# An RWKV block's decay made feature-major with a scan, the state products by two heads in turn, and modulation chunks beside the r, k, v products

## The chip, the cores and the metric

The kernel runs on one core of a Trainium2 chip. The metric is the device time of one execution in microseconds (us); for the kernel before it is given as the median of three runs. TensorE (PE) multiplies matrices, VectorE (DVE), ScalarE (ACT) and GpSimd (POOL) work elementwise, SyncE (SP) issues the DMA transfers. Each engine runs its instructions in the order of its own queue and waits for the others by semaphores.

## The reference

A model block for 512 positions of width 1024: a modulation vector from the condition, a norm, one wide projection, dilated attention and an RWKV-7 mixer side by side, gates, and a convolutional feed-forward; a second block with a mixture of experts follows. The change lies in the RWKV mixer with 16 heads of 64 features, of which this is the part that counts:

```python
z = z + (z_prev - z) * mu
r, k, v, w_low, a_low, g_low = jnp.split(z, [...], axis=-1)
w_log = -jax.nn.softplus(-(w0 + jnp.tanh(w_low) @ w2).astype(f32)) - 0.5
decay = jnp.exp(-jnp.exp(w_log))
a = jax.nn.sigmoid((a0 + a_low @ a2).astype(f32))
kk = heads(k * k_k)
kk = kk / jnp.maximum(jnp.sqrt(jnp.sum(kk * kk, axis=-1, keepdims=True)), 1e-12)

def step(state, inp):
    r_t, w_t, k_t, v_t, aa_t, bb_t = inp
    sa = jnp.einsum('bhvk,bhk->bhv', state, aa_t)
    state = state * w_t[:, :, None, :] + sa[..., None] * bb_t[:, :, None, :] + v_t[..., None] * k_t[:, :, None, :]
    return state, jnp.einsum('bhvk,bhk->bhv', state, r_t)
```

The logarithm of the decay is a constant times (1 + tanh(half of w0 + tanh(w_low) w2)), so inside a chunk of 64 positions the products of decays are exponentials of running sums.

## The kernel before

The sequence of 512 is cut into 8 chunks of 64 positions. `rwkv_quarter(q, fw)` runs four times, each for four heads, which are two halves (`i2`) of 128 features, two heads each. A quarter has four parts.

First its fronts, one for each half. `th` (L610 to L613) holds tanh of `tw` times `w2q` for 512 positions by 256 features, positions on partitions, for the whole quarter: four fp32 products with a row of ones for w0, two ACT tanh, one DVE add of 1. Four fp32 products of `th` with the triangle `tri` give the running sums `cum`, features on partitions, and ACT makes Dp and Dh (their exponentials, L627, L628). One product of `a2q` (rows 64 to 127) gives `ta`. Then come the dense products k, r, v in this order, each 24 fp32r products of 512 columns (a weight is split by `split` into `hi`, a cast on ACT, and `lo`, a subtraction on POOL or DVE in turn). Behind k stand the squares `ksq` and their sums (`a<-c,tmp`), then max, root and reciprocal `rn` (DVE L657, ACT L658, DVE L659), its broadcast (`a<-c,rn`), `kkn` (L673), `ta` (L674), and the tiles AR (L676, L677) and BKf (L675). Sixteen fp32 products of BKf with AR follow, one for each chunk and head, each on 64 rows (`par` 0 or 1), and DVE multiplies them with masks into SA and SB (L691, L692).

Second the chain: the 32x32 blocks go to DRAM and back (`Ad`, `At`), DVE inverts them in 31 steps of two operations, and the inverse goes through DRAM again (`Td`, `TTh`, `Tq`); PE waits for it at `b<-inv`. Third the scan over the 8 chunks, a serial loop in which each chunk has three small groups on PE: `b<-X,SA`, `b<-Ps,TT`, `b<-X,SB`. Fourth the group norm of Y (tile `Ti`, L798 to L806), its transposes (`b<-c,Ti`) and the store.

Other work fills PE: `fw` is a chain of generators, `f_qk`, `f_v` (24 products of 256 columns for each piece, copied out as `stv`) and `f_gate`, that do the dense products of attention and gates; `pull(fw, n)` takes n pieces of it between the scan's steps. `fa` makes the modulation (`ada_group`): a chunk loads 1 MB of raw weight (`raw`, two buffers, shared with the other raw weights) and has eight fp32 products with 32 columns of output and 256 of input (`mm<-raw,c`), plus a DVE add into `rows`. Before, `run_fill` behind each quarter takes the rest of that quarter's `fw` in turn with five pieces of `fa`, for the quarters 1 and 2.

The program order is a list of priorities: a scheduler puts the instructions of each engine in order from it, with its own estimates of when operands are there. So code written behind the quarter stands in the engines' queues beside the chain and the scan of the same quarter, and fronts of the next quarter stand inside the scan. PSUM tiles: tag `a` and `b` three banks each, `mm` two.

Of the kernel before, what the change touches and what calls it, by code (L numbers as in the profile page):

```python
# [20 lines left out]
PVN = [('n1', 8), ('bada', 48), ('bgate', 16), ('mu', 24), ('mul0', 1), ('mul1', 1), ('mul2', 1), ('a0', 8),  # L21
# [28 lines left out]
def constants():  # L50
# [4 lines left out]
    tri = np.where(blk & (p[:, None] <= p[None]), -0.5 * EM5, 0.0)  # L55
# [5 lines left out]
    c1 = np.concatenate([tri, mA, blk, hs2], 1)  # L61
# [29 lines left out]
def layout(inp):  # L91
# [6 lines left out]
           'mul1': mu[3200:3280], 'mul2': mu[3280:3360], 'a0': g['a0'], 'kk': g['k_k'], 'ka': g['k_a'],  # L98
# [26 lines left out]
    A['w2a'] = np.ascontiguousarray(np.concatenate([g['w2'][0], g['w0']], 0))  # L125
# [36 lines left out]
def body(tc, I, O):  # L162
# [4 lines left out]
    with es:  # L167
# [8 lines left out]
        def G(tag="a"):  # L176
            return pp.tile([128, 512], F32, tag=tag, bufs=3, name=tag)
# [4 lines left out]
        def mm(out, l, r, start=True, stop=True):  # L182
            return nc.tensor.matmul(out, l, r, start=start, stop=stop, skip_group_check=True)  # L183

# [313 lines left out]
        c1 = rp.tile([128, 386], F32, name="c1")  # L498
        nc.sync.dma_start(c1, I['c1'])
        tri, mA, blk1, hs2 = c1[:, 0:128], c1[:, 128:256], c1[:, 256:384], c1[:, 384:386]  # L500
        dv = rp.tile([128, 52], F32, name="dv")
        omu, ka2, a0h, rkh, omul = dv[:, 0:24], dv[:, 24:32], dv[:, 32:40], dv[:, 40:48], dv[:, 48:51]
# [3 lines left out]
        nc.vector.tensor_scalar(a0h, V('a0'), 0.5, None, op0=OP.mult)  # L506
        nc.vector.tensor_scalar(rkh, V('rk'), 0.5, None, op0=OP.mult)
# [6 lines left out]
        tw = rp.tile([65, 512], F32, name="tw")  # L514
# [3 lines left out]
        nc.scalar.activation(tw[0:64], wl[0:64], AF.Tanh)  # L518
        nc.gpsimd.memset(tw[64:65], 1.0)
# [79 lines left out]
        def rwkv_quarter(q, fw):  # L599
            T = lambda shape, tag, bufs=1, dt=F32: (rpa if tag in EARLY else rp).tile(list(shape), dt, tag=tag, bufs=bufs, name=tag)  # L600
            w2q = T([65, 256], "w2q")
            nc.sync.dma_start(w2q, I['w2a'][:, 256 * q:256 * q + 256])
# [4 lines left out]
            th = T([128, 4, 256], "th")  # L607
            for t2 in range(2):
                ps = G()
                for t in range(2):  # L610
                    mm(ps[:, 256 * t:256 * t + 256], tw[:, 128 * (2 * t2 + t):128 * (2 * t2 + t) + 128], w2q)
                nc.scalar.activation(th[:, 2 * t2:2 * t2 + 2], ps.rearrange("p (a b) -> p a b", a=2), AF.Tanh, scale=0.5)
            nc.vector.tensor_scalar(th, th, 1.0, None, op0=OP.add)  # L613
# [4 lines left out]
            for i2 in range(2):  # L618
                i = 2 * q + i2
                ii = slice(128 * i2, 128 * i2 + 128)  # L620
                cum = G()
                for t in range(4):
                    mm(cum[:, 128 * t:128 * t + 128], th[:, t, ii], tri)
# [1218 lines left out]
```

## Time and profile before

| | us |
|---|---|
| median of three runs | 2034.93 |
| lowest, highest | 2030.18, 2035.95 |
| the profiled execution | 2040.78 |
| its span, first to last instruction | 2039.0 |
| PE busy | 1932.9 |
| DVE busy | 1146.4 |
| ACT busy | 728.3 |

The mean granted TensorE clock was 0.966 of full speed. RWKV and the fillers run from about 60 to about 740 us; attention, the feed-forward and the second block follow. On the page, the span is cut in 40 slices of 51 us, and each digit is the busy share in tenths; the row PEclk is the clock that PE was granted, in tenths. Matmuls overlap in PE's pipeline, so what a group costs is read from the start of one to the start of the next, not from its duration. An fp32 product is two records. In the rows an idle time in square brackets is the wait of the engine just ahead, with what ended it.

### The profile page before, as it was taken

What the parts mean: (1) busy time and instruction counts of PE and PEld (TensorE: products, weight loads), DVE (VectorE), ACT (ScalarE), POOL (GpSimd) and SP (SyncE); (2) the same over time, 40 slices, a digit from 0 to 9 for tenths busy, and PEclk for the clock granted to TensorE, in tenths of its full rate; (3) what the DMA queues carried; (4) which work ended last, traced back from release to release, by engine and by line L of the source; (5) the groups of instructions that cost most, each with busy time, mean ns of one, the idle gap of its engine ahead of it and who ended that gap; (6) DMA issues with size and microseconds to landing.
All of it is one profiled execution on the core that took longest, in us unless ns stands there. A gap on an engine that the chain in (4) does not pass through costs nothing. (4 is left out here: it accounts for less than half of the span.)

```text
span 2039.0 us, 28480 instructions
## 1 busy us (share of the span) xinstructions
PE 1932.9 (95%) x11085; PEld 1442.3 (71%) x11085; DVE 1146.4 (56%) x2232; ACT 728.3 (36%) x1261; POOL 436.8 (21%) x273
## 2 busy tenths in 40 slices
PE   7999999999999899999999989999999999599997
PEld 4788787787888767777887767777779667444553
DVE  4573573463437354557898873174430562467776
ACT  3533423342343243324333332354332452322222
POOL 1421311220232111131322322221111131122221
PEclk9999999997999999999999999999999899799998
DMA  7233244324234254244655544222233341699994
GB/s 298 78 105 104 80 120 146 117 95 122 92 104 166 81 199 163 95 166 145 199 194 181 181 160 147 92 90 82 89 114 104 98 181 40 241 421 424 424 423 195
DMA packets 100048, 334.11 MB, mean 164 GB/s; under 512 B 30212, under 2 KB 35080, under 8 KB 76360
## 3 DMA queue, kind: packets, MB, share of 16 engines
q1 hardware_dynamic: 97608, 323.89, 44.7%
q0 software_dynamic: 2304, 8.39, 1.1%
q8 instruction: 88, 1.44, 0.3%
q14 instruction: 48, 0.39, 0.1%
HBM read 304.98 MB, written 27.26 MB: 163 GB/s over the span
## 5 line engine op out<-in xcount | busy, mean ns | idle before, releaser
L231 POOL TENSOR_TENSOR lo<-raw,hi 128x1024 fp32r<-128x1024 f32 (+1 forms) x108 | 261.1, 2417 | 904.9 <-ACT hi L228 803.3
L228 ACT CAST hi<-raw 128x1024 fp32r<-128x1024 f32 (+1 forms) x215 | 222.3, 1038 | 368.5 <-PE mm L183 303.0
L183 PE MATMUL mm<-hl,hi 128*128 128x512 f32 x1008 | 333.3, 405 | 0.3 <-ACT stv L584 0.3
L183 PE MATMUL mm<-h,hi 128*128 128x512 f32 x784 | 248.3, 396 | 8.1 <-DVE u L1054 6.0
L231 DVE TENSOR_TENSOR lo<-raw,hi 128x1024 fp32r<-128x1024 f32 (+1 forms) x107 | 140.5, 1313 | 197.9 <-ACT hi L228 196.6
L183 PEld LDWEIGHTS mm<-hl,hi 128*128 128x128 f32 x1008 | 189.6, 191 | 42.1 <-issue 6.3
L183 PE MATMUL mm<-hl,lo 128*128 128x512 f32 x504 | 202.1, 401 | 0.0
L183 PEld LDWEIGHTS mm<-h,hi 128*128 128x128 f32 x784 | 146.5, 189 | 45.4 <-issue 12.3
L356 DVE SCALAR_TENSOR_TENSOR asum<-araw,cv,asum 128x256 f32<-128x256 f32 x224 | 151.5, 680 | 25.7 <-DMA araw<-in_wada 20.7
L183 PE MATMUL mm<-h,lo 128*128 128x512 f32 x392 | 153.9, 393 | 0.0
L183 PE MATMUL mm<-fm,hi 128*128 128x512 f32 x352 | 111.4, 397 | 6.1 <-ACT fm L1058 6.1
L183 PE MATMUL b<-h,hi 128*128 128x512 f32 x368 | 115.8, 392 | 0.0
L183 PE MATMUL mm<-gu,XT 128*64 128x512 f32 x512 | 113.2, 595 | 0.0
L183 PEld LDWEIGHTS mm<-hl,lo 128*128 128x128 f32 x504 | 96.0, 190 | 20.3 <-issue 2.2
L183 PEld LDWEIGHTS mm<-gu,XT 128*64 128x64 f32 x512 | 36.8, 138 | 73.0 <-issue 63.5
L183 PEld LDWEIGHTS mm<-h,lo 128*128 128x128 f32 x392 | 74.2, 189 | 15.8 <-issue 0.2
L183 PEld LDWEIGHTS mm<-fm,hi 128*128 128x128 f32 x352 | 66.7, 191 | 22.1 <-ACT fm L1058 6.5
L183 PEld LDWEIGHTS b<-h,hi 128*128 128x128 f32 x368 | 69.7, 190 | 14.7 <-issue 0.2
L183 PE MATMUL b<-h,lo 128*128 128x512 f32 x184 | 72.2, 392 | 0.0
L183 PE MATMUL mm<-fm,lo 128*128 128x512 f32 x176 | 69.2, 393 | 0.0
L893 ACT ACTIVATE sc<-sc,st 128x512 f32<-128x512 f32 (+3 forms) x96 | 56.3, 588 | 26.6 <-DVE st L891 22.3
L183 PE MATMUL mm<-hi,hl 128*128 128x256 f32 x384 | 57.6, 296 | 2.8 <-ACT stv L584 2.8
(522 smaller groups left out, 3554.1 us busy)
## 6 DMA issues: line engine op xcount, KB each, us to landing
gu<-in_wgu SPq DMA_DIRECT2D x32, 2048.0 KB, 15.0
araw<-in_wada SPq DMA_DIRECT2D x128, 256.0 KB, 3.3
dn<-in_wde SPq DMA_DIRECT2D x32, 1024.0 KB, 14.8
raw<-in_wup SPq DMA_DIRECT2D x22, 1024.0 KB, 4.8
raw<-in_wada SPq DMA_DIRECT2D x16, 1024.0 KB, 5.9
raw<-in_wg SPq DMA_DIRECT2D x16, 1024.0 KB, 5.0
raw<-in_wrkv SPq DMA_DIRECT2D x12, 1024.0 KB, 5.1
raw<-in_wqk SPq DMA_DIRECT2D x12, 1024.0 KB, 4.9
```

The lines of the kernel that those rows point to most:

```text
L183: return nc.tensor.matmul(out, l, r, start=start, stop=stop, skip_group_check=True)
L228: nc.scalar.copy(hi[:, :n], src)
L231: eng.tensor_sub(lo[:, :n], src, hi[:, :n])
L356: nc.vector.scalar_tensor_tensor(a, raw[:, k], c, a, op0=OP.mult, op1=OP.add)
L893: nc.scalar.activation(sc[:, :W], sc[:, :W], AF.Exp, scale=-1.0, bias=st[:, 0:1], accum_out=st[:, 1:2])
```

## The change

Three things.

The decay. `th` for a quarter and the products with `tri` go. Each half has one product of w2q with `tw` (64 rows) into `wps`, features on partitions, put in turn with the product of `a2q` (`in_turn`: each is issued behind the one ahead of it). ACT makes tanh with w0 as its bias, DVE adds 1 over 128x512 and runs a multiply-and-add scan over it with the mask `keep`, which is 0 at each chunk's first position, so that the sum starts anew there (the trace would name it SCALAR_TENSOR_TENSOR `th<-keep,th`). Dp and Dh take the constant as the exponential's scale.

The sixteen products of BKf and AR go through `in_turn` with the two heads alternating throughout.

The modulation's pieces in the quarters 1 and 2 are pulled in the loop over k, r, v, behind k and v of the first half and k, r, v of the second, and no longer by `run_fill`.

```diff
+        def in_turn(calls):
+            i = None
+            for out, l, r, kw in calls:
+                with tc.issue_after(i.ins) if i is not None else nullcontext():
+                    i = mm(out, l, r, **kw)
+            return i
...
-        tw = rp.tile([65, 512], F32, name="tw")
+        tw = rp.tile([64, 512], F32, name="tw")
+
+        keep = rp.tile([128, 512], F32, name="keep")
+        nc.gpsimd.memset(keep, 1.0)
+        nc.gpsimd.memset(keep[:, 0:512:64], 0.0)
...
-        def rwkv_quarter(q, fw):
+        def rwkv_quarter(q, fw, na):
...
-            th = T([128, 4, 256], "th")
-            for t2 in range(2):
-                ps = G()
-                for t in range(2):
-                    mm(ps[:, 256 * t:256 * t + 256], tw[:, 128 * (2 * t2 + t):128 * (2 * t2 + t) + 128], w2q)
-                nc.scalar.activation(th[:, 2 * t2:2 * t2 + 2], ps.rearrange("p (a b) -> p a b", a=2), AF.Tanh, scale=0.5)
-            nc.vector.tensor_scalar(th, th, 1.0, None, op0=OP.add)
...
-                cum = G()
-                for t in range(4):
-                    mm(cum[:, 128 * t:128 * t + 128], th[:, t, ii], tri)
+                wps, aps = G(), G()
+                in_turn([(wps, w2q[:, ii], tw, {}), (aps, a2q[64:128, ii], wl[64:128], {})])
+                cum = T([128, 512], "th")
+                nc.scalar.activation(cum, wps, AF.Tanh, scale=0.5, bias=w0h[:, i:i + 1])
+                nc.vector.tensor_scalar(cum, cum, 1.0, None, op0=OP.add)
+                nc.vector.tensor_tensor_scan(cum, keep, cum, 0.0, OP.mult, OP.add)
...
-                nc.scalar.activation(Dp, c3, AF.Exp)
-                nc.scalar.activation(Dh, c3, AF.Exp, scale=-1.0, bias=eps[:, 1:2])
-                aps = G()
-                mm(aps, a2q[64:128, ii], wl[64:128])
+                nc.scalar.activation(Dp, c3, AF.Exp, scale=-0.5 * EM5)
+                nc.scalar.activation(Dh, c3, AF.Exp, scale=0.5 * EM5, bias=eps[:, 1:2])
...
                         acc = MM()
                         dense(acc, next(rkv_it), H)
+                    pull(fa, na and (1 if i2 or s != 1 else 0))
...
-                    for c in range(4):
-                        for par in range(2):
-                            mm(pA[par][:, 128 * c:128 * c + 128],
-                               BKf[64 * par:64 * par + 64, 4 * c4 + c].rearrange("p a b -> p (a b)"),
-                               AR[64 * par:64 * par + 64, 4 * c4 + c].rearrange("p a b -> p (a b)"))
+                    in_turn((pA[par][:, 128 * c:128 * c + 128],
+                             BKf[64 * par:64 * par + 64, 4 * c4 + c].rearrange("p a b -> p (a b)"),
+                             AR[64 * par:64 * par + 64, 4 * c4 + c].rearrange("p a b -> p (a b)"), {})
+                            for c in range(4) for par in range(2))
...
-            rwkv_quarter(q, fq)
-            run_fill(fq, islice(fa, na))
+            rwkv_quarter(q, fq, na)
+            run_fill(fq)
```

The loop visits s = 1 (k), 0 (r), 2 (v), so `s != 1` in the first half are r and v.

What this does to the engines' queues is seen at three places. The rows below are instructions in the order of one engine (line, operation, output and operands, shape, count of equal neighbours); lines of the changed kernel are up to six higher.

PE, q0, from the first half's AR products to the second half's first products, before; `mm<-hl` are dense products, `hl` the normed input:

```order
L183 MATMUL a<-AR,BKf 128x128 x16
L699 MATMUL a<-c_66,v 128x128 x4
L183 MATMUL mm<-hl,hi 128x512 x2
L183 MATMUL mm<-hl,lo 128x512
...
L712 MATMUL a<-c_66,BKf 128x128 x8
L183 MATMUL a<-c_433,th 128x128 x4
L183 MATMUL a<-wl,a2q 128x512
```

The same place in the changed kernel:

```order
L182 MATMUL a<-AR,BKf 128x128 x9
L182 MATMUL mm<-hl,hi 128x512 x2
L182 MATMUL mm<-hl,lo 128x512
L182 MATMUL a<-AR,BKf 128x128 x7
L704 MATMUL a<-c_66,v 128x128 x4
...
L717 MATMUL a<-c_66,BKf 128x128 x4
L182 MATMUL a<-tw,w2q 128x512
L182 MATMUL a<-wl,a2q 128x512
```

Three dense products now part the AR products, and the pair of w2 and a2 stands where the `th` products and a2 stood.

PE at the end of q0's scan, from the last state products to the transposes of Y (tile Ti), before (between the rows around the dots stand further dense products, 41 in all):

```order
L183 MATMUL b<-X,SB_459 128x64 x2
L183 MATMUL mm<-hl,lo 128x512
L183 MATMUL mm<-hl,hi 128x512 x2
...
L183 MATMUL mm<-hl,hi 128x512
L811 MATMUL b<-c_66,Ti 128x128 x4
L183 MATMUL b<-sg,g2q 128x512 x2
```

and in the changed kernel, complete:

```order
L182 MATMUL b<-X,SB_462 128x64 x2
L182 MATMUL mm<-raw,c_80 32x256 x8
L182 MATMUL mm<-hl,hi 128x512 x2
L182 MATMUL mm<-hl,lo 128x512
L182 MATMUL mm<-hl,hi 128x512 x2
L182 MATMUL mm<-hl,lo 128x512
L182 MATMUL mm<-hl,hi 128x512
L816 MATMUL b<-c_66,Ti 128x128 x4
L182 MATMUL b<-sg,g2q 128x512 x2
```

The dense products here are of v in q1's first half; on ACT the changed kernel has, at this place,

```order
L720 COPY SA_459<-AR 64x8x64 x2
L807 ACTIVATE inv<-Ti 128x1024
L235 CAST hi<-raw 128x1024
L809 ACT_TABLE_LOAD
```

with the square of the norm (`inv<-Ti`) ahead of the cast of v's weights (`hi<-raw`).

PE at the start of q1's second half, before:

```order
L712 MATMUL a<-c_66,BKf 128x128 x8
L183 MATMUL a<-c_433,th 128x128 x4
L183 MATMUL a<-wl,a2q 128x512
L183 MATMUL a<-c_433,tmp 128x2 x4
L183 MATMUL mm<-hl,hi 128x512
L183 MATMUL mm<-hl,lo 128x512
...
L183 MATMUL a<-c_66,rn 64x128 x8
```

and in the changed kernel:

```order
L717 MATMUL a<-c_66,BKf 128x128 x4
L182 MATMUL a<-tw,w2q 128x512
L182 MATMUL a<-wl,a2q 128x512
L182 MATMUL mm<-hl,hi 128x512 x2
L182 MATMUL mm<-hl,lo 128x512
...
L182 MATMUL mm<-raw,c_80 32x256 x8
L182 MATMUL a<-c_433,tmp 128x2 x4
L182 MATMUL a<-c_66,rn 64x128 x8
L182 MATMUL mm<-hl,hi 128x512 x2
```

The sums of squares (`a<-c_433,tmp`) and the broadcast of `rn`, parted by twenty dense products before, are now neighbours behind a chunk of the modulation. In q2's first half the order is the same, chunk, squares, `rn`, and AR follows with one product between.

## Rows read from the trace of the kernel before

**Rows 1.** The page: busy time of PE; PE busy and granted clock in slices

```profile
PE 1932.9 (95%) x11085; PEld 1442.3 (71%) x11085; DVE 1146.4 (56%) x2232; ACT 728.3 (36%) x1261; POOL 436.8 (21%) x273
...
PE   7999999999999899999999989999999999599997
...
PEclk9999999997999999999999999999999899799998
```

**Rows 2.** What PE waited for in 60 to 720 us: total, times, longest

```profile
PE b L183 <- DMA inv<-Td: 8.6, 4, 5.5
...
PE mm L183 <- ACT stv L584: 3.2, 3, 2.2
...
PE b L811 <- DVE Ti L806: 0.8, 1, 0.8
```

**Rows 3.** Timeline of PE, 87.5 to 91.5 us: start, duration, engine, line, operation, records

```profile
88.33 1.06 PE L183 MATMUL a<-c,th 128*128 128x128 f32 x8
89.32 1.12 PE L183 MATMUL a<-wl,a2q 64*128 64x512 f32 x2
90.37 0.50 PE L183 MATMUL mm<-hl,hi 128*128 128x512 f32 x1
90.71 0.39 PE L183 MATMUL mm<-hl,lo 128*128 128x512 f32 x1
90.94 0.63 PE L183 MATMUL mm<-hl,hi 128*128 128x512 f32 x2
```

**Rows 4.** Timeline of PE, 64 to 73 us

```profile
64.17 2.21 PE L183 MATMUL a<-w2q,tw 65*128 65x256 f32 x8 [3.38 <-issue]
65.82 1.41 PE L183 MATMUL mm<-hl,hi 128*128 128x512 f32 x2
```

**Rows 5.** Stretches, PE on tile BKf: window, its length, busy (records), clock, DMA

```profile
109.99:111.07 1.08, 1.08 (x17) 1.00 0.06 23
111.07:111.50 0.43, 0.43 (x7) 1.00 0.00 0
111.50:113.14 1.64, 1.59 (x13) 1.00 0.00 0
```

**Rows 6.** Stretches: length, busy of PE, PEld, DVE, ACT, POOL, then clock, DMA

```profile
308.10:311.50 3.40, 3.40 (x11) 2.53 (x9) 0.48 (x2) 0.00 (x0) 0.00 (x0) 0.50 0.58 229
...
482.20:489.00 6.80, 6.80 (x48) 6.56 (x45) 1.38 (x4) 2.19 (x3) 0.00 (x0) 0.50 0.44 152
492.40:516.30 23.90, 23.90 (x108) 17.38 (x105) 4.59 (x13) 5.61 (x12) 0.00 (x0) 0.50 0.38 134
```

**Rows 7.** Timeline of PE, 304 to 312 us

```profile
305.10 2.21 PE L183 MATMUL b<-inv,SA 32*32 32x32 f32 x64 [1.07 <-DMA inv<-Td]
```

**Rows 8.** Timeline of DVE, 213 to 224 us, q0's norm

```profile
214.25 0.43 DVE L792 TENSOR_TENSOR Ti<-b,Ps 64x256 f32<-64x256 f32 x1 [0.29 <-PE b L183]
...
222.24 1.23 DVE L806 TENSOR_TENSOR Ti<-Ti,mn 128x1024 f32<-128x1024 f32 x1
```

**Rows 9.** Timeline of ACT, 213 to 224 us

```profile
219.26 1.04 ACT L228 CAST hi<-raw 128x1024 fp32r<-128x1024 f32 x1
```

**Rows 10.** Timeline of ACT, 218 to 258 us, q1's second half

```profile
244.41 1.28 ACT L627 ACT_TABLE_LOAD   x1
245.70 0.60 ACT L627 ACTIVATE Dp<-a 128x512 f32<-128x512 f32 x1
...
247.48 1.28 ACT L658 ACT_TABLE_LOAD   x1
```

**Rows 11.** Timeline of DVE, 218 to 258 us, q1's two halves

```profile
233.76 0.75 DVE L673 SCALAR_TENSOR_TENSOR kkn<-k,pv,a 128x512 f32<-128x512 f32 x1 [0.58 <-PE a L183]
...
236.35 0.17 DVE L677 COPY AR<-kkn 128x8 f32<-128x8 f32 x1
...
240.68 1.28 DVE L706 TENSOR_TENSOR BKf<-BKf,Dp 128x512 f32<-128x512 f32 x2
...
251.08 1.87 DVE L663 SCALAR_TENSOR_TENSOR tmp<-r,dv,km 128x512 f32<-128x512 f32 x1 [1.87 <-POOL km L649]
```

More of the change, by code (lines that the diff above doesn't have):

```diff
@@ L19 @@
 MAGIC = 1.5 * 2.0 ** 23
-PVN = [('n1', 8), ('bada', 48), ('bgate', 16), ('mu', 24), ('mul0', 1), ('mul1', 1), ('mul2', 1), ('a0', 8),
+PVN = [('n1', 8), ('bada', 48), ('bgate', 16), ('mu', 24), ('mul0', 1), ('mul1', 1), ('mul2', 1), ('a0', 8), ('w0', 8),
        ('kk', 8), ('ka', 8), ('rk', 8), ('lw', 8), ('lb', 8), ('n2', 8), ('cw0', 44), ('cw1', 44), ('cw2', 44),
@@ L54, in constants @@
     blk = (p[:, None] // 64 == p[None] // 64)
-    tri = np.where(blk & (p[:, None] <= p[None]), -0.5 * EM5, 0.0)
     s = p % 64
@@ L60, in constants @@
     c0 = np.concatenate([ident, ones], 1)
-    c1 = np.concatenate([tri, mA, blk, hs2], 1)
+    c1 = np.concatenate([mA, blk, hs2], 1)
     r, i = p // 32, p % 32
@@ L97, in layout @@
     src = {'n1': g['norm1_w'], 'bada': g['b_ada'], 'bgate': g['b_gate'], 'mu': mu[:3072], 'mul0': mu[3072:3200],
-           'mul1': mu[3200:3280], 'mul2': mu[3280:3360], 'a0': g['a0'], 'kk': g['k_k'], 'ka': g['k_a'],
+           'mul1': mu[3200:3280], 'mul2': mu[3280:3360], 'a0': g['a0'], 'w0': g['w0'], 'kk': g['k_k'], 'ka': g['k_a'],
            'rk': g['r_k'], 'lw': g['lnx_w'], 'lb': g['lnx_b'], 'n2': g['norm2_w'], 'cw0': g['conv_w'][0, 0],
@@ L124, in layout @@
     A['wg'] = _chunks(np.stack([t[j] for j in range(8) for t in (ga, gb)]), 2)
-    A['w2a'] = np.ascontiguousarray(np.concatenate([g['w2'][0], g['w0']], 0))
+    A['w2'] = np.ascontiguousarray(g['w2'][0])
     A['a2'] = g['a2'][0]
@@ L497, in body @@
         rp = rw.enter_context(tc.tile_pool(name="rw", bufs=1))
-        c1 = rp.tile([128, 386], F32, name="c1")
+        c1 = rp.tile([128, 258], F32, name="c1")
         nc.sync.dma_start(c1, I['c1'])
-        tri, mA, blk1, hs2 = c1[:, 0:128], c1[:, 128:256], c1[:, 256:384], c1[:, 384:386]
-        dv = rp.tile([128, 52], F32, name="dv")
-        omu, ka2, a0h, rkh, omul = dv[:, 0:24], dv[:, 24:32], dv[:, 32:40], dv[:, 40:48], dv[:, 48:51]
+        mA, blk1, hs2 = c1[:, 0:128], c1[:, 128:256], c1[:, 256:258]
+        dv = rp.tile([128, 60], F32, name="dv")
+        omu, ka2, a0h, rkh, omul, w0h = dv[:, 0:24], dv[:, 24:32], dv[:, 32:40], dv[:, 40:48], dv[:, 48:51], dv[:, 52:60]
         nc.vector.tensor_scalar(omu, V('mu'), -1.0, 1.0, op0=OP.mult, op1=OP.add)
@@ L506, in body @@
         nc.vector.tensor_scalar(a0h, V('a0'), 0.5, None, op0=OP.mult)
+        nc.vector.tensor_scalar(w0h, V('w0'), 0.5, None, op0=OP.mult)
         nc.vector.tensor_scalar(rkh, V('rk'), 0.5, None, op0=OP.mult)
@@ L517, in body @@
         shift(accs[0], 128, V('mul0'), omul[:, 0:1], wl)
-        nc.scalar.activation(tw[0:64], wl[0:64], AF.Tanh)
-        nc.gpsimd.memset(tw[64:65], 1.0)
+        nc.scalar.activation(tw, wl[0:64], AF.Tanh)
         for s in range(2):
@@ L597, in f_gate @@
                     yield
-        def rwkv_quarter(q, fw):
+        def rwkv_quarter(q, fw, na):
             T = lambda shape, tag, bufs=1, dt=F32: (rpa if tag in EARLY else rp).tile(list(shape), dt, tag=tag, bufs=bufs, name=tag)
-            w2q = T([65, 256], "w2q")
-            nc.sync.dma_start(w2q, I['w2a'][:, 256 * q:256 * q + 256])
+            w2q = T([64, 256], "w2q")
+            nc.sync.dma_start(w2q, I['w2'][:, 256 * q:256 * q + 256])
             a2q = T([128, 256], "a2q")
```

## The prediction, made before the changed kernel ran

> **What bounds the kernel now.** I read the page's busy line and slices first: TensorE (PE) is busy for 95% of the span, and its tenths stand at 9 from the second slice to the last but one with three dips [rows 1]. The reader should then look at what PE waits for in 60 to 720 us, where the changed code runs: the longest entry is 8.6 us in four waits, for the inverse of the 32x32 blocks that comes back by DMA at the end of DVE's chain, and the next that the change touches is 3.2 us for `stv`, the copy behind a group of f_v [rows 2]. So in these 660 us PE's own work is the time, and a transfer or a faster DVE can give back some 15 us at most. Third, the granted clock: PE's two levels are 2.4 and 1.2 GHz, and three stretches show 0.50, one of them 23.9 us long with PE busy throughout [rows 6]. Work there costs double. The rest, 740 us onward, is the same program in both kernels; I take it as unchanged.
>
> **Decay: what goes and what comes.** Before, each quarter has four products of w2 (1.65 us from the first to the next group's start, [rows 4]), and each half a group of `th` products, 88.33 to 89.32 = 0.99 us, and one `a2` product, to 90.37 = 1.05 us [rows 3]. Per quarter 1.65 + 2 x 0.99 + 2 x 1.05 = 5.73, for four 22.9 us. After, each half has one w2 and one a2 product of 512 columns each, on rows 0 to 63 and 64 to 127. Whether they run together is the question. The nearest row is the product of AR and BKf: while the two heads alternate, 8 instructions of 128 columns take 1.08 us [rows 5], what 4 instructions of the same columns on all rows take in [rows 3]. The pair then costs 1.05, with a switch 1.1, and where the order splits it (once, in q0's scan, by state products) 2.1: 7 x 1.1 + 2.1 = 9.8. **Saving 13.1 us**; if they don't overlap it is 22.9 - 8 x 2.1 = 6.1, and 15 at best. On DVE the +1 over 128x1024 becomes two over 128x512, and two scans come. No row shows a scan: I bound it by an elementwise operation of 128x512 at 0.75 and by the slowest such at 1.87 [rows 11], and take 1.2, between the two. It lies beside PE's dense products wherever they stand between the pair and the first use of Dp, and in the open at the start of q1's and q2's second half, below.
>
> In the Trainium skill, "DVE: opcode table, instruction layouts, handler registers and perf-mode slots", paragraph Feedback, the scan runs at half throughput; doubling a plain operation's 0.75 would give an estimate of 1.5 and add 0.3 to each of those two places, 0.6 us to the sum. No run shows it yet.
>
> **AR by two heads in turn.** Before, the sixteen products come as 1.08 us alternating, then 0.43 and 1.64 for the other eight, four of one head and four of the other [rows 5]. After, nine come, some dense products, then seven: the ninth by itself about 0.2, the seven at the alternating rate 0.95. So 3.15 becomes 1.08 + 0.2 + 0.95 = 2.25 plus 0.2 for breaking in and out of the dense products: 0.6 to 0.7 saved, eight times, 4.8 us. But DVE now does the first BKf product (half of the 1.28 us of two, [rows 11]) ahead of the last four masks, so the blocks leave for DRAM some 0.6 us later, and that chain is the one that PE waits for at `b<-inv` [rows 2]: 4 x 0.6 = 2.4 given back. **Net -2.4 us** (-4.8 if the inverse has slack, 0 if none of the saving reaches its start).
>
> **The modulation's chunks leave the scans.** Their work on PE is the same wherever they stand, so moving them is worth only what it does to waits and clock. In q2's scan before, PE has those chunks, small state products and hardly any dense products from 492.4 to 516.3, all at 0.50 [rows 6]. After, dense products of f_v and f_gate stand in that place. At full clock those 23.9 us of work take half: **-12 us**, at least 0. The 482.2 to 489.0 stretch behind the inverse's wait stays. In q1's and q2's scans PE waited for `stv` [rows 2] where the chunks and f_v share the two mm banks; of 3.2 I take **-2 us**.
>
> **What their new place costs.** The dense products that fill the scans were taken from the joints between the quarters, and there PE now meets chains that were covered. Four places, by the order:
>
> (1) End of q0's scan. From the sum into Y at 214.25 to the last product of the norm at 222.24 + 1.23 = 223.47 is 9.2 us [rows 8], and before 41 dense products, 0.23 each [rows 3], lay in it; the wait there was 0.8 us [rows 2]. After, one chunk (1.0) and seven dense products (1.6) lie there, and these seven need a cast (1.04, before at 219.26, [rows 9]) that ACT now does behind the norm's square. 9.2 - 2.6 = 6.6 open, less what was open before and what the shorter DVE queue gives: **+5.5**.
>
> (2) Second half of q1. Between the decay pair and the squares' products stand six dense products and a chunk, 2.4 us with the pair's own 1.1 = 3.5. ACT needs in the same time a table load (1.28), the tanh, ta, k, km2, Dp, Dh and the square, at some 0.6 each [rows 10]: 5.5 to 6. Open: 2.3. The next products, `rn`, follow without any dense product in between, and behind the square ACT loads the sqrt table again, 1.28 [rows 10], of which the squares' products cover 0.9: with max, root and reciprocal 1.0 open. Then r's lo part stands on DVE behind kkn (0.75, [rows 11]): 1.5. **+4.8** (2.7 if the table is there and the split is early, 5.5).
>
> (3) First half of q2: chunk, squares, `rn`, and straight to AR. The root's chain is open as in (2), with a DVE product of up to 1.87 [rows 11] ahead of the reciprocal: 2.4. Then kkn to the copy of AR, 233.76 to 236.35 + 0.17 = 2.8 [rows 11], has only one product of 1.1 in front of AR (before, eight dense products with it): 2.4 with the hops. **+4.9** (2.5 to 6).
>
> (4) Second half of q2, like (2): **+4.6** (2.7 to 5.5).
>
> Sum 19.8, from 13.4 to 22.5. **The clock behind these waits.** A wait of 1.07 us for the inverse [rows 7] was followed by 3.4 us at 0.50 from 308.1 on, and the inverse's wait in q2 by 6.8 us from 482.2 on [rows 6]. I take 3.4 us for each of the four places, at half speed a loss of 1.7: **+6.8** (0 to 13.6).
>
> **Sum.** -13.1 - 2.4 - 12 - 2 + 19.8 + 6.8 = -2.9 us. The profiled run took 2040.78 us, its span 2039.0, and stands 5.9 above the median of the three runs, 2034.93; a difference of -2.9 on either puts the median at 2032.
>
> **Rivals.**
> A, the joints cost less. If the clock stays at 1.0 behind the four waits (-6.8), and they take their lower bounds, 13.4 (-6.4), the sum is -16 and the time 2019. For it: a wait of 0.8 us before Ti [rows 2] had no slow slice behind it [rows 1]. Against: the order of ACT and DVE is fixed, so the waits at the joints are not a matter of luck.
>
> B, slower: the clock falls at the joints for longer. Chunk, squares and `rn` products of few columns now follow one another with waits between them, which is what the 23.9 us at 0.50 consisted of [rows 6]. If each joint brings 6.8 us at half clock (+6.8 over the forecast) and the 6 us or so of thin products at the two starts of second halves run at half clock as well (+6), the sum is -2.9 + 12.8 = +10, 2045. It decides from the point where the half-clock time gained at the joints passes the 24 us saved in q2's scan.
> The Trainium skill, "TensorE: Matmul & The Clock Gate", section HAM oscillation, says that waits between groups of matmuls let the clock fall, so that each next group starts at the slow level. By that rule all four joints pay, and B's first half holds. The stretch from 308.1 [rows 6] agrees for a wait of 1.07 us [rows 7].
>
> C, the pair doesn't run together. The two products of a pair are 512 columns long and only two, where AR's alternated eight times; then 13.1 becomes 6.1 and the time is 2039. For it: the eight AR products that came as four and four took 1.64 us in their main part, so two in a row of one head did not overlap with the other's [rows 5].
>
> D, the change does not lift the clock in q2's scan: state products of 64 columns stay and dense ones of 256 columns come between. Then 12 are missing: 2044. Against: q0's scan, with dense products between the same state products, keeps the clock at 9 tenths or more in its slices [rows 1].
>
> **How the numbers follow.** About 0.3%, 6.1 us, is what a measurement of this kernel tells from no change, so the bounds are 2028.8 and 2041.0. The forecast, 2032 with 2026 to 2038 by its single terms, has 0.44, of which 0.10 lies below 2028.8; A 0.24, B 0.16, C 0.08, D 0.08. Faster: 0.10 + 0.24 = 0.34. Same: 0.34 + 0.08 (C) = 0.42. Slower: 0.16 + 0.08 = 0.24. The range 2017 to 2045 leaves out about a third of A and half of B, and half of D's upper part.
>
> **What would show it.** In the profile after: the pair's two products starting within 0.1 us of each other and done in 1.1; AR in two runs, 1.1 and 0.95; q2's scan at a granted clock of 1.0; PE waits of 5 to 6 us at the end of q0's scan (before the transposes of Ti), and of 2 to 5 us ahead of `rn` and AR in q1's second half and both of q2's, each followed by 0.50 in the clock. The prediction is wrong if the joints show no waits, if the pair runs in 2.1, if half-clock time at the joints passes 20 us, or if the part from 740 us on differs by more than 3 us.

## The result and the profile after

The changed kernel is slower: median 2064.67 us of six runs (2057.4 to 2072.0) against 2034.3 of six runs of the kernel before, a ratio of 1.0133 with a 95% interval of 1.0093 to 1.0173. That is some 27 us by the ratio and 30 by the two medians. The forecast was 2032 with a range to 2045. The profiled execution took 2058.02 us, its span 2056.2. The first attention product (`po<-PT`), where the unchanged rest of the program begins, starts at 767.26 us, before at 743.93: 23.3 us later. The rest takes 1289.0 us after it, before 1295.0, with the same instructions: PE is at half clock, that is at a granted clock of 0.50, for 60.7 us of the rest, before for 82.1. The rest of the program isn't steady. It took 1295.3 us in a second trace of the changed kernel, and 1288.7 to 1302.1 over all traces of this document.

First the page of the changed kernel: PE is busy for 6.9 us less than in [rows 1] and a smaller share of a longer span; in the first half of the span the busy share falls in the fifth and the ninth slice, and the clock in the fifth, ninth, fourteenth and fifteenth.

```profile
PE 1926.0 (94%) x11005; PEld 1426.2 (69%) x11005; DVE 1169.6 (57%) x2245; ACT 729.5 (35%) x1261; POOL 436.6 (21%) x274
...
PE   7999799989999999999999989989999999699997
...
PEclk9999899989999889999999999999999999799999
```

What PE waited for in 60 to 760 us (total, times, longest), to be held against [rows 2]:

```profile
PE a L182 <- ACT tmp L652: 7.3, 3, 2.8
PE mm L182 <- ACT hi L235: 6.5, 2, 6.0
PE b L182 <- DMA inv<-Td: 6.1, 3, 4.4
PE a L182 <- DVE AR L683: 5.3, 4, 2.0
PE a L182 <- DVE bv L685: 5.3, 2, 2.7
PE mm L182 <- ACT stv L595: 5.0, 3, 3.3
PE a L182 <- DVE rn L665: 3.3, 4, 1.6
PE mm L182 <- DVE lo L238: 3.0, 2, 2.8
PE b L816 <- DVE Ti L811: 2.8, 3, 1.8
```

The wait for the inverse, the longest entry before, is now third. Above and around it stand waits inside the fronts: for the squares (`tmp` L652), a cast (`hi`), AR, `bv` (the bonus sums times v), `rn` and `lo`. Over the stretch from 60 us to the start of attention, before and then after (length, busy us of PE, PEld, DVE, ACT, POOL, then clock, DMA), PE is busy for the same time, and its idle time is 47.8 us instead of 24.1:

```profile
60.00:743.90 683.90, 659.78 (x4257) 537.95 (x4256) 358.19 (x710) 258.26 (x411) 144.87 (x84) 0.96 0.34 109
60.00:767.30 707.30, 659.50 (x4180) 528.16 (x4179) 377.62 (x710) 256.05 (x404) 144.44 (x84) 0.93 0.33 105
```

Then the stages of the changed kernel in the same columns, without those that the text doesn't read. The boundaries of all are the first w2 product of q1 (180.70), q1's AR products (235.01, 269.41), its inverse (324.28), its transposes of Y (385.07), the same for q2 (414.01, 461.11, 514.91, 573.55), q3's inverse (685.70) and attention.

```profile
180.70:235.01 54.31, 46.38 (x261) 32.77 (x260) 24.27 (x47) 18.59 (x31) 10.36 (x9) 0.91 0.21 75
235.01:269.41 34.40, 29.70 (x172) 21.24 (x172) 20.48 (x30) 17.43 (x24) 8.87 (x5) 0.85 0.39 131
269.41:324.28 54.87, 48.91 (x365) 45.50 (x364) 38.89 (x83) 14.29 (x24) 9.86 (x4) 0.96 0.45 132
...
414.01:461.11 47.10, 40.24 (x220) 28.45 (x221) 21.75 (x33) 18.72 (x26) 11.43 (x6) 0.86 0.41 140
461.11:514.91 53.80, 48.57 (x287) 41.80 (x286) 40.53 (x83) 13.89 (x21) 9.85 (x4) 0.97 0.43 131
514.91:573.55 58.64, 56.80 (x494) 51.65 (x495) 26.17 (x45) 22.24 (x43) 5.08 (x3) 0.97 0.19 61
...
685.70:767.26 81.56, 79.55 (x582) 60.70 (x582) 32.30 (x74) 26.82 (x53) 7.26 (x4) 0.82 0.27 91
```

and of the kernel before the two stages between the AR products, q2's scan and the last stage:

```profile
236.75:257.63 20.88, 19.68 (x124) 15.12 (x123) 14.50 (x25) 11.86 (x17) 6.27 (x4) 1.00 0.20 60
...
405.01:430.37 25.36, 24.71 (x146) 19.50 (x146) 13.41 (x25) 14.21 (x20) 8.63 (x5) 1.00 0.17 51
...
480.73:553.30 72.57, 70.51 (x523) 60.74 (x524) 27.66 (x49) 23.32 (x43) 7.45 (x4) 0.79 0.32 105
...
670.55:743.93 73.38, 70.69 (x589) 55.13 (x589) 32.82 (x80) 27.80 (x57) 7.45 (x4) 0.96 0.32 107
```

| stage | before, us (clock) | after, us (clock) |
|---|---|---|
| to q1's first w2 product | 124.54 (0.96) | 120.70 (0.96) |
| to q1's first AR | 52.21 (1.00) | 54.31 (0.91) |
| q1's first to second AR | 20.88 (1.00) | 34.40 (0.85) |
| to q1's inverse | 47.47 (1.00) | 54.87 (0.96) |
| q1's scan | 62.04 (0.97) | 60.79 (0.93) |
| to q2's first AR | 37.87 (1.00) | 28.94 (1.00) |
| q2's first to second AR | 25.36 (1.00) | 47.10 (0.86) |
| to q2's inverse | 50.36 (1.00) | 53.80 (0.97) |
| q2's scan | 72.57 (0.79) | 58.64 (0.97) |
| to q3's inverse | 117.25 (1.00) | 112.15 (1.00) |
| to attention | 73.38 (0.96) | 81.56 (0.82) |

q2's scan gave what was forecast, 13.9 us, with its clock back from 0.79 to 0.97. (What stands in a stage differs between the kernels: two chunks left this one and 18 dense products came in.) The stages from the first to the second AR of q1 and of q2 lost 13.5 and 21.7 us, of which the moved chunks and dense products are about half by their counts (two chunks of 1.07 us and 21 dense products of 0.23 more in q1, three and 31 in q2). Waits and a clock of 0.85 and 0.86 are the other half. The way from q1's second AR to its inverse lost 7.4, and the last stage 8.2.

The second front of q1, timeline of PE in the changed kernel, shows how one joint looks:

```profile
241.15 0.69 PE L182 MATMUL a<-tw,w2q 64*128 64x512 f32 x1
241.15 0.69 PE L182 MATMUL a<-wl,a2q 64*128 64x512 f32 x1
241.68 0.59 PE L182 MATMUL a<-tw,w2q 64*128 64x512 f32 x1
241.69 0.59 PE L182 MATMUL a<-wl,a2q 64*128 64x512 f32 x1
242.20 0.73 PE L182 MATMUL mm<-hl,hi 128*128 128x512 f32 x2
...
243.79 1.07 PE L182 MATMUL mm<-raw,c 128*32 128x256 f32 x16
247.50 1.64 PE L182 MATMUL a<-c,tmp 128*128 128x2 f32 x8 [2.64 <-ACT tmp L652]
249.87 1.97 PE L182 MATMUL a<-c,rn 128*64 128x128 f32 x16 [0.73 <-DVE rn L665]
252.41 1.22 PE L182 MATMUL mm<-hl,hi 128*128 128x512 f32 x2 [0.57 <-ACT hi L235]
...
270.50 0.50 PE L182 MATMUL mm<-hl,hi 128*128 128x512 f32 x1
273.65 0.48 PE L182 MATMUL a<-AR,BKf 64*128 64x128 f32 x2 [2.64 <-DVE bv L685]
```

The pair of w2 and a2 starts together and is done in 1.05 us, as forecast. Then come a chunk, a wait for ACT, the squares, a wait for the root, `rn`, a wait for a cast; and at the ninth AR product one of 2.64 us for `bv`, which no step of the prediction had. On DVE the modulation's own last operation (`ada`, L310, 2.10 us from 270.04) stands ahead of v and `bv` there, and in q2's second half likewise (2.10 us from 461.74).

### The profile page after: what moved, and what is told of

It reads as the page before. It is cut to its first block, busy times and chain, and to the rows that moved or that the text cites. A ratio compares the mean times of both kernels' runs of the same rounds, so it can differ in the third digit from the quotient of the medians.

```text
span 2056.2 us, 28313 instructions
## 1 busy us (share of the span) xinstructions
PE 1926.0 (94%) x11005; PEld 1426.2 (69%) x11005; DVE 1169.6 (57%) x2245; ACT 729.5 (35%) x1261; POOL 436.6 (21%) x274
## 5 line engine op out<-in xcount | busy, mean ns | idle before, releaser
L182 PE MATMUL mm<-hl,hi 128*128 128x512 f32 x1008 | 347.1, 418 | 11.0 <-ACT hi L235 6.5
L363 DVE SCALAR_TENSOR_TENSOR asum<-araw,cv,asum 128x256 f32<-128x256 f32 x224 | 154.2, 691 | 23.4 <-DMA araw<-in_wada 18.8
L734 DVE TENSOR_TENSOR Ti<-Ti,Ps 64x31 f32<-64x31 f32 (+15 forms) x124 | 58.4, 471 | 4.2
```

What stands on the lines that cost most here:

```text
L363: nc.vector.scalar_tensor_tensor(a, raw[:, k], c, a, op0=OP.mult, op1=OP.add)
L734: nc.vector.tensor_sub(Ti[:, 0:s + 1, s + 1:32], Ti[:, 0:s + 1, s + 1:32], m)
```

## The experiments

Ratios are to the kernel before on the same chip, with 95% intervals; 1% is 20 us. The median of the kernel before lay between 2034.3 and 2042.2 us on these chips, so kernels are compared by their ratios rather than by their times. In this section the chain is the inverse's, as in the part on the kernel before.

| kernel | ratio | interval |
|---|---|---|
| all three parts (the change) | 1.0133 | 1.0093 to 1.0173 |
| the change again | 1.0136 | 1.0081 to 1.0192 |
| decay and AR, chunks as before | 0.9970 | 0.9938 to 1.0001 |
| chunks moved, nothing else | 1.0241 | 1.0188 to 1.0295 |
| decay alone | 0.9997 | 0.9966 to 1.0028 |
| AR in turn alone | 1.0104 | 1.0047 to 1.0160 |
| the change with spare products | 1.0144 | 1.0093 to 1.0194 |
| chunks in the chain, nothing else | 0.9938 | 0.9908 to 0.9968 |
| the same with AR | 0.9969 | 0.9943 to 0.9995 |
| the same with decay | 0.9897; 0.9920 | 0.9868 to 0.9926; 0.9892 to 0.9947 |
| the same with decay and AR | 0.9956; 0.9956 | 0.9937 to 0.9976; 0.9928 to 0.9985 |
| the same with decay ahead and AR | 0.9922 | 0.9890 to 0.9954 |
| the same with decay ahead | 0.9911 | 0.9879 to 0.9943 |
| chunks at q1's joints, q2's in the chain | 1.0035 | 1.0002 to 1.0068 |
| chunks at q2's joints, q1's in the chain | 1.0041 | 1.0011 to 1.0071 |

**The parts apart.** Theory 1: the chunks' new place makes the loss. Theory 2: the decay's longer way through ACT and DVE does.

Chunks put back:

```diff
-                    pull(fa, na and (1 if i2 or s != 1 else 0))
-            run_fill(fq)
+            run_fill(fq, islice(fa, na))
```

> The changed kernel with the modulation's chunks put back behind the quarters (the decay by scan and the AR products in turn stay). Theory 1, the moved chunks make the loss (they take the dense products out of the joints, PE waits there and its clock falls): this kernel is free of it and keeps the saving of the decay products, 13 us less about 4 us for the squares of q1's second half, which now stand right behind the w2 and a2 pair: 2020 to 2026. Half-clock time between 60 and 740 us 45 to 60 us as before, PE waits 20 to 26 us in all. Theory 2, the decay's longer chain through ACT and DVE (tanh, add, scan, exponentials) makes the waits wherever the chunks stand: 2045 to 2060, with waits on tmp of over 6 us and half-clock time over 70 us.

Measured 2034.65, ratio 0.997: 33 us (1.6%) better than the change, so theory 2 is out as the main cause. But it was expected at 2020 to 2026; decay and AR brought 0.3%, not 0.6. PE's idle time was 25.5 us, as expected, but the half-clock time 73 us instead of 45 to 60, with 27 us of it in q2's scan.

The kernel before with the reverse of this edit, that is the chunks' move alone:

> The kernel before with only the modulation's chunks moved beside r, k, v. Theory 1 (the chunks make the loss): 2055 to 2075, that is what the change lost plus what decay and AR give, with PE waits in 60 to 760 us of 40 us or more and half-clock time of 75 us or more. Theory 2 (the decay's chain makes the waits): 2025 to 2040, since here the decay is ready a quarter ahead; half-clock time falls to some 30 us because q2's scan keeps its clock.

2090.72, ratio 1.0241, beyond what theory 1 expected. PE's idle time in the RWKV part is 48.1 us, as in the change, and about 117 us of that part go at half clock; among the waits stand 8.3 us for `stv` and 7.8 for Ti. Here the decay is ready ahead, and the loss is larger. One part of the expectation failed: q2's scan, with no chunk in it, ran at half clock from 519.9 us on for 27.3 us, from within a wait of 4.07 us for `stv`. So moving the chunks out of a scan doesn't by itself keep its clock.

Decay alone (the `tri` and `th` lines of the diff, chunks and AR as before), then AR in turn alone:

> The kernel before with only the decay by scan. By the prediction's term 13 us are saved on PE, of which 4 go to a wait ahead of the squares in q1's second half: 2022 to 2027 by theory 1. By theory 2: 2045 or more. Beside the run with decay and AR it shows what AR in turn is worth: if more than 2 us, AR's saving reaches the end; if nothing or less, it is given back through the masks and the inverse's chain.

2037.05, ratio 0.9997: neither theory's number. Its profile has two stretches of 27 and 20 us at half clock in the scans of q1 and q2, where the chunks still stand (stage, PE busy, then clock at the end):

```profile
308.20:335.60 27.40, 26.89 (x162) 18.63 (x159) 6.79 (x17) 7.73 (x14) 2.35 (x1) 0.50 0.43 159
496.00:516.50 20.50, 19.34 (x90) 13.91 (x90) 4.25 (x11) 3.27 (x8) 0.45 (x1) 0.50 0.42 147
```

> The kernel before with only the AR products in turn. By the prediction 2.4 us faster (4.8 saved on PE, 2.4 given back by the later masks): 2030 to 2034. If the broken rows of dense products or a wait for the third PSUM bank cost more than that: 2035 to 2040.

2058.05, ratio 1.0104, a miss: slower than either expectation. Its profile has two such stretches of 30.7 us:

```profile
315.30:346.00 30.70, 29.78 (x170) 21.41 (x168) 4.94 (x15) 7.64 (x14) 2.36 (x1) 0.50 0.27 102
496.20:526.90 30.70, 28.01 (x167) 20.43 (x166) 4.99 (x14) 6.37 (x15) 0.00 (x0) 0.50 0.32 109
```

Before, q1's scan lost it for 3.4 us only [rows 6]. With a small edit in the fronts, q1's scan with chunks in it fell to half clock as well. So the parts can't be priced with the chunks in the scans.

**Chunks in the chain.** To price them with the clock quieter, the chunks were placed among dense products while DVE inverts:

```diff
+            for j in range(na):
+                pull(fw, 12 if j == 0 else 4)
+                pull(fa, 1)
             At = T([64, 32, 32], "inv")
```

> The kernel before with only the chunks in the inverse's chain. Theory: the 24 us at half clock in q2's scan go, so 8 to 12 us faster than before, ratio 0.994 to 0.996; the distance to the kernel with decay and AR as well is what these two are worth once the clock holds, 10 to 16 us. Rival: same as before, 1.000, when the chunks among the chain's products bring waits of their own (raw weights by DMA, rows on DVE between the inverse's steps).

2025.0, ratio 0.9938: 0.6% from the chunks' place alone, a little more than was expected.

> Decay by scan and AR in turn, with the modulation's chunks pulled in the inverse's chain: behind the second half of q1 and q2 twelve pieces of f_qk, f_v, then one chunk, four pieces, one chunk and so on. Chunks then stand among dense products while DVE inverts, the joints have their dense products as before, and the scans of q1 and q2 hold dense products only. Theory (the clock in the scans and the waits at the joints decide, and the decay's 13 us are real): half-clock time in 60 to 760 us 25 to 40 us, PE waits 20 us, time 20 to 30 us below before, ratio 0.985 to 0.990. If the 13 us of the decay never reach the end: ratio 0.993 to 0.997, like the kernel with the chunks behind the quarters.

2025.85, ratio 0.9956: short of the 0.985 to 0.990, no better than the same without decay and AR. The clock wasn't as quiet as expected: 60 us at half clock instead of 25 to 40. Which of the two eats the gain was asked by leaving out one at a time: first the decay, then AR in turn.

> The kernel before with AR in turn and the chunks in the inverse's chain. AR in turn alone cost 1.0 per cent with the chunks behind the quarters, in a trace with 31 us at half clock in q1's scan and again in q2's. Theory: that was the clock in the scans, not AR; then this kernel is 0 to 4 us faster than the one with the chunks in the chain and the AR order of before, ratio 0.992 to 0.996. Rival: AR in turn costs by itself (broken dense groups, later masks): 10 us or more slower than that kernel, ratio 1.000 or more.

2028.7, ratio 0.9969: 0.3% slower than without AR in turn, between theory and rival, but the intervals overlap, so a cost isn't shown here.

> Decay by scan at each half's start, AR in the order of before, chunks in the inverse's chain. Theory: as the kernel with AR in turn, within 4 us, ratio 0.993 to 0.997; the distance to the kernel with the decay computed ahead is the price of the uncovered chain, 4 to 10 us. Rival: no distance, the waits at q1's second half are covered by time that would be lost at the inverse anyway.

2016.23, ratio 0.9897, the best of all. Against the kernel without the decay (0.9938, on another chip) it is worth 0.4%, 8 us of the 13.1, though the intervals overlap. Timed side by side in five rounds:

> Decay by scan, AR in turn, chunks in the chain, timed again beside the same with the AR order of before. If AR in turn costs: 6 to 12 us slower than that one (their separate medians were 2025.9 and 2016.2). If that distance was the chips' and the clock's chance: within 3 us of each other. By the prediction it would be 2.4 us faster.

> Decay by scan, the AR order of before, chunks in the chain: the best so far, ratio 0.9897. Expected again 0.988 to 0.993, 16 to 24 us below before.

2025.79 against 2019.14, ratios 0.9956 and 0.9920: with the decay by scan the kernel with AR in turn is some 7 us slower; the intervals overlap, the two separate comparisons agree in sign. But little of that lies where AR stands. In the two pairs of traces attention starts only 0.8 and 4.3 us later with AR in turn; the other 8.8 and 6.3 us fall in the unchanged rest, which has 90.5 and 83.3 us at half clock against 64.4 and 73.5. Whether the order of AR brings that isn't shown. What the traces do show is where the saving went. Timeline of PE in q1's second half, with AR in turn:

```profile
243.60 1.09 PE L182 MATMUL a<-c,rn 128*64 128x128 f32 x16
252.59 2.04 PE L182 MATMUL a<-tmp,c 128*128 128x512 f32 x2 [4.95 <-DVE tmp L668]
255.41 1.86 PE L182 MATMUL a<-AR,BKf 64*128 64x128 f32 x18
```

and with the AR order of before:

```profile
247.19 1.09 PE L182 MATMUL a<-c,rn 128*64 128x128 f32 x16
253.84 1.10 PE L182 MATMUL a<-tmp,c 128*128 128x512 f32 x2 [2.16 <-DVE tmp L668]
```

With AR in turn PE is 3.6 us ahead at `rn`, then waits 4.95 us instead of 2.16 for the bonus product that DVE and POOL make, and the clock falls (0.57 granted over 249 to 257 us), so that the products behind it take double. The saving on PE was real and was handed to a wait.

**The decay ahead.** That wait comes from the decay's way through ACT, so it was computed for both halves at the quarter's start (two buffers for `th` and `ta`):

```diff
+            for i2 in range(2):
+                wps, aps = G(), G()
+                in_turn([(wps, w2q[:, ii], tw, {}), (aps, a2q[64:128, ii], wl[64:128], {})])
...
+                cums.append(cum)
+                tas.append(ta)
```

> Decay by scan, AR in turn, chunks in the inverse's chain, and the w2 and a2 pairs, tanh, add and scan of both halves computed at the quarter's start instead of at each half's (two buffers for them; tanh of w_low is kept in place of w_low, the mask in bf16, to make room). Theory: in the kernel with the chunks in the chain what is left of the change's cost is the decay's chain through ACT and DVE, uncovered at q1's second half, where PE waited 4.9 us ahead of the bonus product. With it a quarter ahead, PE's waits fall by 4 to 6 us and the kernel is 4 to 10 us faster than that one: ratio to before 0.991 to 0.994, PE waits below 20 us, no wait over 2 us in q1's fronts. Rival: the decay's products are worth nothing at the end whatever covers them: 0.994 to 0.997.

> The same with the AR products in the order of before. The distance of the two is what AR in turn is worth with all else quiet. By the prediction 2.4 us (4.8 saved on PE, 2.4 given back by the later masks): this kernel 0 to 5 us slower than the one with AR in turn. Rival (AR in turn costs): this kernel 2 us or more faster.

2022.62 and 2023.15, ratios 0.9922 and 0.9911. With AR in turn the ratio is 0.3% lower than without the decay ahead, but the intervals overlap; the 4.9 us wait is gone, but one for AR of 3.7 us came, and PE's idle time is 22.4 us where less than 20 was expected. With the AR order of before it doesn't help: there the uncovered chain had no price, as the rival said. AR in turn is worth nothing here.

**The clock behind the waits.** The change with 68 dense products whose result nobody uses, put where PE waited:

```diff
+        def spare(n, i):
+            acc = G("b")
+            for j in range(n):
+                with tc.issue_after(i.ins):
+                    i = mm(acc, H[j % 8][0][:, 0:128], H[j % 8][0], start=(j == 0), stop=(j == n - 1))
+            return i
```

> The changed kernel with 68 spare dense products (their result is used by nobody) put where PE waited: 24 before the transposes of Y at the end of q0's scan, 10 behind the w2 and a2 pair of the second halves of q1 and q2, 6 between the squares and rn in all four fronts of these quarters. The order of all other instructions of PE stays. At full clock they are 68 x 0.23 = 15.4 us of work. Theory 1 (the granted clock that falls behind the waits costs about half of the loss): half-clock time between 60 and 760 us falls from 96 to 60 us or less, and the kernel, with more work, is 8 to 15 us faster than the changed one: 2050 to 2057 where before is 2034, a ratio to before of 1.008 to 1.012 or less. Rival (the waits alone are the loss, the clock follows chance): the same or up to 6 us slower than the changed kernel, ratio 1.013 to 1.017, since spare products that overrun a wait add time.

2067.39, ratio 1.0144: the rival's number. Half-clock time fell only to 75 us, not to 60, and the order didn't stay quite the same: at the end of q0's scan v's seven products now stand behind the transposes of Y. There the filling worked. The stretch 205 to 232 us, with the spare products and then in the change itself (the clock stands behind the five busy times):

```profile
205.00:232.00 27.00, 23.96 (x141) 16.59 (x140) 13.37 (x20) 9.83 (x14) 7.97 (x7) 1.00 0.34 111
```

```profile
205.00:232.00 27.00, 19.07 (x107) 11.91 (x106) 11.54 (x18) 9.72 (x13) 7.82 (x7) 0.81 0.30 105
```

The clock stays at 1.00 there instead of 0.81, and although PE has 30 products (6.8 us) more, q1's first AR comes 1.5 us sooner, counted from q1's first w2 product (52.86 against 54.31). So the waits there could be filled for nothing; whether the 1.5 us come from the clock or from the new order, this run can't tell. In q1's second half the clock fell all the same for 10 us, and with 16 spare products the way from the first to the second AR took 39.03 us instead of 34.40. Over the whole stretch attention starts at 767.67 us, in the change at 767.26: the spare work was paid for by 10.2 us less idle time and by 20 us less at half clock. My theory 1, that a quieter clock would make the kernel 8 to 15 us faster, isn't borne out. Waits and clock aren't two separate losses here: where PE runs faster it may wait longer for the same chain.

**Chance or order.** The changed kernel once more, without an edit.

> The changed kernel once more, on the chip of the others. Theory (the slow clock behind the joints belongs to the order, not to chance): half-clock time in 60 to 767 us again 85 to 105 us, with stretches of 3 us or more behind the same five joints (some 210, 248, 275, 439, 466 us), waits 45 to 50 us, ratio 1.010 to 1.016. Rival (chance): half-clock time below 70 us or at other places, ratio within 0.5 per cent of 1.

2059.58, ratio 1.0136, and 85 us at half clock, with stretches at 210, 245, 272, 320, 412, 436 and 463 us, all within 3.3 us of the first trace's; one of 3.4 us at 227 did not come again. So these belong to the order.

**One quarter at a time.** The pull at the joints for one quarter, in the chain for the other:

```diff
-                    pull(fa, na and (1 if i2 or s != 1 else 0))
+                    pull(fa, q == 1 and (1 if i2 or s != 1 else 0))
...
+            for j in range(0 if q == 1 else na):
+                pull(fw, 12 if j == 0 else 4)
+                pull(fa, 1)
```

> Decay by scan and AR in turn; q1's chunks beside its r, k, v products as in the change, q2's in the inverse's chain. With all chunks in the chain the ratio to before was 0.9956, with all at the joints 1.0133, 36 us apart. Theory (each joint is paid by itself: its waits and the slow clock behind them): about 60 per cent of that here, since q1 has the end of q0's scan besides its two fronts, 20 to 23 us, ratio 1.004 to 1.008. Rival (one place decides, say q2): within 8 us of one of the two ends.

> The mirror: q2's chunks at its joints, q1's in the chain. Theory: about 40 per cent of the 36 us, 13 to 17 us, ratio 1.001 to 1.005, and the excess of the two mixed kernels over the one with all chunks in the chain adds up to that of the changed kernel within 8 us. Rival: the two do not add up.

2043.61 and 2047.31, ratios 1.0035 and 1.0041. Over the kernel with all chunks in the chain (0.9956) that is 16 and 17 us, together 33; the change stands 36 over it. Each of the two has an uncertainty of some 7 us. Within it the quarters' losses add up; q1's share, expected at 20 to 23, is no larger than q2's. PE's idle time says the same: 35.0 and 35.4 us, between 23.4 with all chunks in the chain and 47.8 in the change.

## Why the prediction was wrong

PE's time from 60 us to attention can be split in three: its work as it would be at full clock, its idle time, and what the slow clock adds. The last is an estimate: half of PE's busy time in the half-clock stretches, which is 50.5 us of 51.1 before and 86.1 us of 95.2 after. It says what the slow clock took, and not what a steady clock would give back. The forecast's terms fall in the same three (of AR's -2.4, 4.8 are work saved and 2.4 a longer wait).

| | forecast, us | measured, us |
|---|---|---|
| work: decay, AR | -17.9 | -18.2 |
| PE's waits: joints, `stv`, inverse | +20.2 | +23.7 |
| slow clock | -5.2 | +17.9 |
| sum (rounded) | -2.9 | +23.3 |

So the work was right, the waits were nearly right in their sum, and the step that failed is the clock.

**The decay's products: right.** The pair takes 1.06 us at six of the seven places where it stands together and 1.13 at one, forecast 1.1, so rival C falls. One scan takes 1.225 us, taken as 1.2. The estimate of 1.5 from the Trainium skill's half throughput ("DVE: opcode table, instruction layouts, handler registers and perf-mode slots", paragraph Feedback) was too high here. Of the 13.1 us, 4 to 8 reach the end with the chunks in the chain (0.9938 to 0.9920 and 0.9897, the intervals overlapping), and none was measurable when they lie in the scans.

**AR in turn: the size was right on PE, the net was not.** Nine products and seven take 1.3 and 1.1 us. But the order gave it back: the ninth product needs a PSUM bank that `bv` reads, and `bv` stands behind the modulation's sum and v in DVE's queue (2.64 and 2.65 us in q1's and q2's second halves); and PE, ahead of the bonus product, waited longer. No pair of runs shows a gain from AR in turn beyond its intervals: with the decay by scan and the chunks in the chain it is some 7 us slower, most of that in the unchanged rest; with the decay ahead it is about even; with the chunks as before it stands 0.3% ahead (0.9970 against 0.9997). The prediction's 2.4 us gain had priced the masks and the inverse only.

**q2's scan: right in this kernel.** -12 was forecast, the stage lost 13.9 us; rival D falls for the change. With the chunks' move alone it would have held, since there this scan stayed at half clock.

**The waits at the joints: right in place, in part by luck.** Forecast were four places with 19.8 us. (1) The end of q0's scan waited 5.98 us for the cast, forecast 5.5, and another 1.91 for the squares of q1's first half. (2) q1's second half waited 2.64 for the squares, 0.73 for `rn`, 0.57 and more for the split, and 2.64 for `bv`: 7 against 4.8. (3) q2's first half, 1.61 for `rn` and 1.90 for AR: 3.5 against 4.9. (4) q2's second half, 2.77, 0.74, 2.78 for `lo` and 2.65 for `bv`: 8.9 against 4.6. Besides, 3.3 us for `stv` in q1's chain, where a gain of 2 had been taken; against that, the waits for the inverse fell from 8.6 to 6.1 us.

At (1) the number is luck: it came from the norm's chain and ACT's order, but the wait ended otherwise. The rows, of PE, SP, ACT and PE, then SP's wait ahead of the load:

```profile
206.18 1.07 PE L182 MATMUL mm<-raw,c 128*32 128x256 f32 x16
207.31 0.33 SPq L229 DMA_DIRECT2D raw<-in_wrkv  x1
212.13 1.04 ACT L235 CAST hi<-raw 128x1024 fp32r<-128x1024 f32 x1 [0.75 <-DMA raw<-in_wrkv]
213.23 1.22 PE L182 MATMUL mm<-hl,hi 128*128 128x512 f32 x2 [5.98 <-ACT hi L235]
216.78 0.74 PE L816 MATMUL b<-c,Ti 128*128 128x128 f32 x4
...
SPq L229 <- PE mm L182: 25.5, 1, 25.5
```

The moved chunk held one of the two `raw` buffers. v's weights were loaded only when the chunk's products had read it, landed 4.8 us later, and were cast in 1.04. The norm was done at 216.34, so with earlier weights a wait for Ti might have stood there instead. At three more places the load of the next weights is issued right behind a chunk (244.92, 407.43, 435.45 us) and the cast waits for it (1.73, 1.75 and 0.64 us). No run gave the chunks a buffer of their own, so what the shared buffers cost isn't measured.

**The clock behind them: the step that failed.** I took four drops of 3.4 us, 14 in all, for a loss of 6.8. In the fronts and at the end of q0's scan there were seven of 3.4 to 10.2 us, 41 in all; by the estimate above they cost 16.4 us. The last stage, q3's scan and the way to attention, had no term in the sum: it has 31 us at half clock instead of 7, which is 11.7 us more. At q1's inverse 10 us stand where 3.4 had been. Half-clock time between 60 us and attention rose from 51 to 95 us, where the sum had 24 fewer in q2's scan and 14 more at the joints. At the joints that is rival B's place, for which the text had 0.16 and a time of 2045; the joints' 41 us passed its point, the 24 us saved in q2's scan. B's comparison with q2's scan misread the row, though: there PE was busy for all of the 23.9 us [rows 6], with no waits between. Two of the signs of being wrong came: the half-clock time at the joints (41 us, the sign was 20) and the rest (6 us off, the sign was 3). The second moves by as much between two traces of the changed kernel.

The section of the Trainium skill that stood beside B ("TensorE: Matmul & The Clock Gate", HAM oscillation) says that waits between groups bring the slow clock back each time. The repeat run agrees for the joints, where the drops come at the same places; the stretches of 20 to 31 us in the scans, with PE busy for 91 to 98% of them, are another case.

What the runs show as the cause is the chunks' new place: putting them back or into the chain takes the loss against the kernel before away, and moving them alone makes one. How much of it the clock would give back by itself stays open, since a faster PE may wait instead, as the run with spare products showed.

Open too is the last stage, which the change hardly touches. It takes 81.6 us at a clock of 0.82, before 73.4 at 0.96, and 81.4 at 0.84 in the best kernel; over all other traces it takes 75.8 to 85.8. No run tells why it is quick in the kernel before, of which there is one trace.

The kernel that beats both the one before and the change has the decay by scan, the AR order of before and the chunks in the chain: 2016.23 and 2019.14 us in its two comparisons, ratios 0.9897 and 0.9920.

## What to carry to other kernels

A filler has two prices: its own work, which is the same wherever it stands, and that of the work which it pushes out of a place where that covered a chain. Before moving one, list for each place that loses dense products which chain lay under them, down to who reads the PSUM bank that the next product needs and which buffer the filler holds, and put the filler where a long chain on another engine still leaves plenty of dense work beside it. And price a saving on the bound engine only with what the next operand's maker does: an engine that arrives sooner may just wait longer, and here lost its clock there (0.57 over 8 us). Price the clock in every stage, also in those that the edit doesn't touch.

## What the hardware showed that I had not expected

Scans with many products of 64 to 256 columns ran at 1.2 GHz for 20 to 31 us with PE busy for 91 to 98% of the time, or kept 2.4 GHz: q1's scan kept it but for 3.4 us before, and lost it with AR in turn alone or the decay alone; q2's lost it with chunks in it and, in the run that only moved them, without them. The places of the drops belong to the order of a kernel: in two traces of the best kernel they begin at 161, 322, 489, 643, 673 and 721 us, within 1 us of each other.
